# A hybrid attention, recurrence and expert block on one core: GpSimd's large two-operand operations go to VectorE

## The chip, the core and the metric

The kernel runs on one core of a Trainium2 chip, in one launch. The metric is the device time of that launch in microseconds (us). The engines are named as the profile names them: PE is TensorE, DVE VectorE, ACT ScalarE, POOL GpSimd, SP SyncE. The kernel before takes 1131.45 us, the median of three runs (1130.12 to 1132.07).

## What is computed

The reference is one layer over 272 tokens (16 learned meta tokens and 256 of the input) of width 1024, all in float32:

```python
h = layer_norm(concat([meta, x]), ln_emb_g, ln_emb_b)
qa, ka, va, qb, fb, ib, gb = split(h @ w_in)                  # 1024 x 3584
ya = diff_attention(qa, ka, va, lam, subln_g, ...)            # 4 heads, rotary, chunk-causal
yb = hgrn2(qb, fb, ib, gb, lb, norm_g)                        # 4 heads, gated linear recurrence
h = layer_norm(2**0.25 * h + concat([ya, yb]) @ w_out, ln1_g, ln1_b)
ffn = moe(h, ...)                                             # top 4 of 32 experts, clamped SwiGLU
return layer_norm(2**0.25 * h + ffn, ln2_g, ln2_b)[16:]
```

The weights of the 32 experts are 403 MB, and every expert has tokens, so all of them are read once.

## The kernel before

**The mixer stage.** `w_in` comes in 28 pieces and `w_out` in 8, each 128x1024 float32. `split` (L173) makes two float32r parts of a piece: ScalarE rounds it (`hi`, L178), and a second engine subtracts (`lo`, L180). That engine is VectorE for the even pieces from 4 on, and GpSimd for the others, 20 of 36. When `lo` is made, the piece's buffer is free, and the SP queue fetches the piece four further on (L183). There are three buffers for `hi` and for `lo`, so piece i+3 can be rounded when TensorE is done with piece i. `project` (L313) multiplies a piece with the 272 tokens in 24 matmuls. In between, by a list of steps written out by hand (`STEPS`, L50), stand the pieces of the recurrence (`diagonal`, `level 0` to `level 7`, `meta`), of the attention (`rope`, `scores`, `turn`, `out_a`), the norms of the heads (`norm`), and `mix`, which multiplies their outputs with the pieces of `w_out`.

The order of TensorE's instructions is that of the list. The order on the other engines is made by a scheduler, which places each instruction by its own estimate of when it can run; on the chip every engine then runs its queue in that order and waits where the head of the queue waits.

**What the change touches in it.** `split` (L180). `router_fold` (L276), which makes the low part of the experts' biases. `residual` (L291 and L292), which scales and shifts the two halves of the tokens, 128x1024 each, with rows eg and eb. `hg_level` (L418), which multiplies neighbouring decays into those of the next level; TensorE's L408 of the next level needs what L416 leaves. `rope` (L483), the product with the cosines. `affine` (L679 and L680), gain and shift of the norm ahead of the experts: whole rows (128x1024) for tokens 0 to 127, half rows (128x512) for tokens 128 to 255. Some small GpSimd operations of `hg_level` (L437, L439), the spreading of the bias selectors (L762) and two operations of the last norm stay on GpSimd.

**From the router to the experts.** `total1`, `turn1`, `logits`, `choose`, `affine`, `position` and `hot1` norm the tokens, choose experts and make the one-hot matrix G; `gather` (L715) multiplies G with the normed tokens, and the first expert's matmuls (L779) follow.

**The experts.** Each expert has six chunks of weights of 2 MB. Ten chunk buffers are there, six of them lent to the mixers as scratch at first. The SP queue issues all transfers in program order: ten chunks before the first expert, each when its buffer is free, the eleventh when the first expert's first chunk has been used, and so on.

Of the kernel before, what the change touches and what calls it, by code (L numbers as in the profile page):

```python
# [11 lines left out]
F32 = mybir.dt.float32  # L12
# [4 lines left out]
OP = mybir.AluOpType  # L17
PSUM = mybir.MemoryType.PSUM if hasattr(mybir, "MemoryType") else bass.MemoryType.PSUM

P = 128  # L20
# [3 lines left out]
L = T + NM  # L24
# [18 lines left out]
E_ROT, E_COS = 0, 128  # L43
# [85 lines left out]
def build(ctx, tc, x, meta, consts_d, mixc_d, vecs_d, rows_d, win_d, wout_d, wr_d, br_d, bgu_d, bdn_d, wexp_d, out):  # L129
    nc = tc.nc  # L130
# [17 lines left out]
    def bank(tag):  # L148
        return ps.tile([P, 512], F32, name="ps_" + tag, tag=tag, bufs=4 if tag == "s" else 2)

    def t1(name, shape=(P, L), dt=F32):
        return cpool.tile(list(shape), dt, name=name, tag="t1", bufs=T1)

    def t4(name, shape=(P, D), dt=F32):
        return cpool.tile(list(shape), dt, name=name, tag="t4", bufs=T4)


    h = cpool.tile([P, 2, D], F32, name="h")
    con = cpool.tile([P, NC_CONST], F32, name="con")
    vec = cpool.tile([P, NC_VEC], F32, name="vec")  # L160
    mixc = pool.tile([P, NC_MIX], F32, name="mixc")
# [4 lines left out]
    def fetch(i):  # L166
        t = pool.tile([P, 1024], F32, name="wraw", tag="raw", bufs=RAW)
        nc.sync.dma_start(t, win_d[i] if i < 28 else wout_d[i - 28])
        wraw[i] = t
# [3 lines left out]
    def split(i):  # L173

        raw = wraw.pop(i)
        hi = wpool.tile([P, 1024], F32R, name="whi", tag="hi", bufs=SPL)
        lo = wpool.tile([P, 1024], F32R, name="wlo", tag="lo", bufs=SPL)
        nc.scalar.copy(hi, raw)  # L178
        eng = nc.gpsimd if i < 3 or i % 2 else nc.vector
        eng.tensor_tensor(lo, raw, hi.bitcast(F32), op=OP.subtract)  # L180
        parts[i] = (hi, lo)
        if i + RAW < 36:
            fetch(i + RAW)  # L183
# [18 lines left out]
    bgu = cpool.tile([P, 2, 512], F32R, name="bgu")  # L202
# [5 lines left out]
    def row_bcast(r, name):  # L208
        t = t4(name)
        nc.sync.dma_start(t, bass.AP(tensor=rows_d.tensor, offset=rows_d.offset + r * D, ap=[[0, P], [1, D]]))  # L210
        return t
# [17 lines left out]
    for i in range(2):  # L229
        split(i)  # L230
# [34 lines left out]
    def router_fold(half):  # L265

        b = bank("g")
        if half == 0:
            nc.sync.dma_start(mixc, mixc_d)
            for k in range(KT):  # L270
                nc.tensor.matmul(b[0:1, 0:NE], vec[:, V_B1 + k:V_B1 + k + 1], wr[:, k, :], start=(k == 0),
                                 stop=(k == KT - 1))
            braw = t4("braw", (P, 2, 512))
            nc.sync.dma_start(braw, bgu_d)
            nc.scalar.copy(bgu, braw)
            nc.gpsimd.tensor_tensor(bgu[64:P], braw[64:P], bgu[64:P].bitcast(F32), op=OP.subtract)  # L276
            nc.vector.tensor_tensor(br, b[0:1, 0:NE], br, op=OP.add)
            nc.vector.tensor_tensor(wr, wr, vec[:, V_G1:V_G1 + 8][:, :, None].to_broadcast([P, KT, NE]), op=OP.mult)
            return
        nc.tensor.matmul(b[:, 0:NE], ones[0:1, :], br, start=True, stop=True)  # L280
        for k in range(KT):
            nc.tensor.matmul(b[:, NE:2 * NE], ones, wr[:, k, :], start=(k == 0), stop=(k == KT - 1))
        nc.vector.tensor_copy(brb, b[:, 0:NE])
        nc.vector.scalar_tensor_tensor(wr, b[:, None, NE:2 * NE].to_broadcast([P, KT, NE]), -1.0 / D, wr, op0=OP.mult,
                                       op1=OP.add)

    def residual():
        eg, eb = row_bcast(0, "eg"), row_bcast(1, "eb")
        rows["g1"], rows["b1"] = row_bcast(2, "g1"), row_bcast(3, "b1")
        for a in range(2):  # L290
            nc.gpsimd.tensor_tensor(h[:, a, :], h[:, a, :], eg, op=OP.mult)  # L291
            nc.gpsimd.tensor_tensor(h[:, a, :], h[:, a, :], eb, op=OP.add)  # L292

    rc, rings = [0], []

# [101 lines left out]
    def hg_level(lv):  # L397
        Kmf = Km.rearrange("p h t -> p (h t)")
        ATv = ATd.rearrange("p h a t -> p (h a) t")
        m = 1 << lv  # L400
        nb = T * 4 // (2 * m)
        Qv = Qf.rearrange("p (n u m) -> p n u m", u=2, m=m)
        Kv = Kf.rearrange("p (n u m) -> p n u m", u=2, m=m)
        b = bank("s")
        if m <= 64:
            for i in range(8):
                n0 = i * (64 // m)
                nc.tensor.matmul(b[:, i * 64:(i + 1) * 64], Kf[:, i * P:(i + 1) * P],  # L408
                                 Qv[:, n0:n0 + 64 // m, 1, :], start=True, stop=True)
        else:  # L410
            for hh in range(4):
                nc.tensor.matmul(b[:, hh * P:(hh + 1) * P], Kx[:, hh, 0:P], Qx[:, hh, P:T], start=True, stop=True)
        Tv = st["T"].rearrange("p (n u) -> p n u", u=2)
        nc.vector.tensor_tensor(Qv[:, :, 1, :], Qv[:, :, 1, :], Tv[:, :, 0:1].to_broadcast([P, nb, m]), op=OP.mult)
        if m <= 64:
            nc.vector.tensor_tensor(Kv[:, :, 0, :], Kv[:, :, 0, :], Tv[:, :, 1:2].to_broadcast([P, nb, m]), op=OP.mult)  # L416
            Tn = Tns[lv % 2][:, 0:nb]
            nc.gpsimd.tensor_tensor(Tn, Tv[:, :, 0], Tv[:, :, 1], op=OP.mult)  # L418
            st["T"] = Tn
        bv = b.rearrange("p (i t) -> p i t", t=64)  # L420
        if m <= 16:
            msk = mixc[:, E_MSK + lv * 64:E_MSK + (lv + 1) * 64].bitcast(I32)
            dst = ATv.rearrange("p i (n u m) -> p i n u m", u=2, m=m)[:, :, :, 1, :]
            nc.vector.copy_predicated(
                dst, msk.rearrange("p (n m) -> p n m", m=m)[:, None, :, :].to_broadcast([P, 8, 64 // m, m]),
                bv.rearrange("p i (n m) -> p i n m", m=m))
        elif m <= 64:
            for q in range(64 // m):
                nc.scalar.copy(ATv[q * 2 * m:q * 2 * m + m, :, q * 2 * m + m:(q + 1) * 2 * m],
                               bv[q * 2 * m:q * 2 * m + m, :, q * m:(q + 1) * m])  # L430
        else:
            nc.scalar.copy(ATx.rearrange("p h t -> p (h t)"), b)
        if m <= 8:
            nbm = 64 // (2 * m)
            Kmv = Kmf.rearrange("p (n u m) -> p n u m", u=2, m=m)
            Tmv = st["Tm"].rearrange("p (n u) -> p n u", u=2)
            nc.gpsimd.tensor_tensor(Kmv[:, :, 0, :], Kmv[:, :, 0, :], Tmv[:, :, 1:2].to_broadcast([P, nbm, m]), op=OP.mult)  # L437
            Tn = Tmns[lv % 2][:, 0:nbm]
            nc.gpsimd.tensor_tensor(Tn, Tmv[:, :, 0], Tmv[:, :, 1], op=OP.mult)  # L439
            st["Tm"] = Tn  # L440
# [36 lines left out]
    def rope(key, dst, m, n):  # L477
        s = rp.pop(key)
        c = bank("g")
        nc.tensor.matmul(c[:, 0:n], mixc[:, E_ROT:E_ROT + P], s[:, 0:n], start=True, stop=True)  # L480
        t = t1("rt")
        nc.vector.tensor_tensor(t[:, 0:n], c[:, 0:n], mixc[:, E_SIN + L - n:E_SIN + L], op=OP.mult)
        nc.gpsimd.tensor_tensor(s[:, 0:n], s[:, 0:n], mixc[:, E_COS + L - n:E_COS + L], op=OP.mult)  # L483
        nc.vector.tensor_tensor(dst[:, m, :], s[:, 0:n], t[:, 0:n], op=OP.add)

    os = {}
# [108 lines left out]
    def close():  # L595
        rawst.close()
        rings.append(ctx.enter_context(tc.tile_pool(name="ring2", bufs=1)))

    do = dict(project=lambda i: project(i, *posts[i]), split=split, prefetch=prefetch, fold=router_fold, residual=residual,
              diagonal=hg_diag, lam=lam, level=hg_level, meta=hg_meta, out_a=out_a, out_b=out_b, norm=fin, scores=scores,  # L600
              turn=a_turn, values_a=lambda m: v_turn("a", m), values_b=lambda m: v_turn("b", m), begin=begin, mix=mixin,
# [65 lines left out]
    g1, b1 = rows["g1"], rows["b1"]  # L667

    def affine(a):
        mu, rs = mus[a]  # L670
        ha = h[:, a, :]
        nmr = small.tile([P, 1], F32, name="nmr")
        nc.vector.scalar_tensor_tensor(nmr, mu, -1.0, rs, op0=OP.mult, op1=OP.mult)
        c0 = 512 if a else 0
        if a:
            nc.vector.scalar_tensor_tensor(ha[:, 0:c0], ha[:, 0:c0], mu, g1[:, 0:c0], op0=OP.subtract, op1=OP.mult)
            nc.vector.scalar_tensor_tensor(ha[:, 0:c0], ha[:, 0:c0], rs, b1[:, 0:c0], op0=OP.mult, op1=OP.add)
        nc.scalar.activation(ha[:, c0:], ha[:, c0:], AF.Identity, bias=nmr, scale=rs)
        nc.gpsimd.tensor_tensor(ha[:, c0:], ha[:, c0:], g1[:, c0:], op=OP.mult)  # L679
        nc.gpsimd.tensor_tensor(ha[:, c0:], ha[:, c0:], b1[:, c0:], op=OP.add)  # L680

    def weigh(a):
        nm = small.tile([P, 1], F32, name="nm")
# [499 lines left out]
```

## Time and profile before

| what | value |
|---|---|
| median of three runs | 1131.45 us |
| the profiled execution, its own time | 1132.66 us |
| its span, from the first instruction to the last | 1130.8 us |
| busy: PE, DVE, ACT, POOL | 1007.2, 337.3, 177.2, 99.2 us |
| bytes moved | 428.44 MB, mean 379 GB/s |
| mean granted TensorE clock | 0.963 |

The span is cut here in stages: the mixers up to about 183 us, the way from the router to the first expert up to 208 us, the experts, and the last norm. A busy share over the whole span hides that: GpSimd is busy for 99.2 us, nearly all of it in the first 200. The granted clock is a share of full speed; 1.0 is 2.4 GHz and 0.5 is 1.2 GHz.

### The profile page before, as it was taken

The page shows a single profiled execution, that of the slowest core. Times are in us where ns is not written, and L with a number is a line of the kernel's source. Part 1 is how long each engine was busy: PE and PEld are TensorE (multiplying, and loading weights), DVE is VectorE, ACT ScalarE, POOL GpSimd, SP SyncE. Part 2 cuts the span into 40 slices and gives each one's busy share as a digit, 9 for nine tenths or more (in the row PEclk, how much of TensorE's full clock was granted, in tenths as well). Part 3 has the DMA queues.
Part 4 walks back from the last instruction along what each step waited for, and adds up shares of the span by engine and source line. Part 5 has one row for each costly group of instructions (what it writes and reads, how often), then busy time and mean ns, then how long its engine had stood idle before and what let it go on. Part 6 is the DMA issues. An engine that isn't in the chain of part 4 may idle for free.

```text
span 1130.8 us, 14815 instructions
## 1 busy us (share of the span) xinstructions
PE 1007.2 (89%) x6066; PEld 525.7 (46%) x6067; DVE 337.3 (30%) x721; ACT 177.2 (16%) x394; POOL 99.2 (9%) x91
## 2 busy tenths in 40 slices
PE   5989898999769999999999999999976699866995
PEld 5988777443225534444444444444421345312432
DVE  6685878312102321222121222122220013200114
ACT  4424564111001001110110001000100001000102
POOL 3653314000000000000000000000000000000001
PEclk9999999999889999999999999999988899988998
DMA  6753468899999999999999999999999999999993
GB/s 216 268 216 109 160 223 304 340 416 400 426 428 427 427 429 427 427 427 427 428 427 426 428 429 427 427 428 428 428 426 427 428 428 429 424 429 427 428 409 129
DMA packets 37022, 428.44 MB, mean 379 GB/s; under 512 B 4388, under 2 KB 4772, under 8 KB 12758
## 3 DMA queue, kind: packets, MB, share of 16 engines
q1 hardware_dynamic: 36322, 426.71, 90.6%
q8 instruction: 50, 0.82, 0.3%
q10 hardware_dynamic: 628, 0.74, 0.2%
q14 instruction: 22, 0.18, 0.0%
HBM read 426.38 MB, written 1.05 MB: 378 GB/s over the span
## 4 chain that ended last, share of the span: by engine, by line
PE 71%; DMA 14%; DVE 6%; ACT 1%; issue 1%; POOL 0%; DVEq 0%; ACTq 0%; POOLq 0%
PE ps_pj L779 21%; DMA wchunk<-in_wexp 14%; PE ps_pj L793 10%; PE ps_s L715 5%; PE ps_pj L864 5%; PE ps_pj L319 4%; PE ps_s L828 4%; PE ps_pj L836 4%; PE ps_pj L828 4%; PE ps_s L897 3%; PE ps_pj L876 2%; PE ps_g L752 1%; PE ps_pj L774 1%; PE ps_s L408 1%; DVE acc L898 1%
## 5 line engine op out<-in xcount | busy, mean ns | idle before, releaser
L779 PE MATMUL ps_pj<-wchunk,XT 128*64 128x512 f32 x1088 | 245.2, 597 | 0.0
L742 DVE TENSOR_SCALAR g<-ps_pj 128x256 f32<-128x256 f32 x52 | 22.1, 425 | 512.5 <-PE ps_pj L779 243.6
L864 PE MATMUL ps_pj<-wchunk,XT 128*32 128x512 f32 x768 | 113.4, 685 | 39.2 <-DMA wchunk<-in_wexp 39.2
L779 PEld LDWEIGHTS ps_pj<-wchunk,XT 128*64 128x64 f32 x1088 | 73.4, 137 | 137.9 <-issue 137.6
L793 PE MATMUL ps_pj<-wchunk,at 128*64 128x256 f32 x1088 | 123.7, 382 | 1.6 <-DVE at L754 1.6
L743 ACT ACTIVATE sgm<-g 128x256 f32<-128x256 f32 x58 | 24.2, 416 | 497.8 <-DVE g L742 497.8
L793 PEld LDWEIGHTS ps_pj<-wchunk,at 128*64 128x64 f32 x1088 | 75.8, 137 | 43.0 <-issue 3.2
L319 PE MATMUL ps_pj<-c,whi 128*128 128x272 f32 (+1 forms) x420 | 84.8, 296 | 0.7 <-DVE c L241 0.4
L762 POOL CAST sel<-sels 128x128 fp32r<-128x128 f32 (+2 forms) x30 | 10.5, 349 | 841.9 <-PE ps_g L752 248.9
L864 PEld LDWEIGHTS ps_pj<-wchunk,XT 128*32 128x32 f32 x768 | 27.5, 122 | 118.0 <-issue 64.0
L715 PE MATMUL ps_s<-G,h 128*128 128x128 f32 (+1 forms) x480 | 61.7, 290 | 15.2 <-DVE G L697 13.9
L876 PE MATMUL ps_pj<-wchunk,at 128*32 128x256 f32 x768 | 58.1, 447 | 17.2 <-DMA wchunk<-in_wexp 8.3
L715 PEld LDWEIGHTS ps_s<-G,h 128*128 128x128 f32 x480 | 58.7, 203 | 27.2 <-DVE G L697 24.4
L319 PEld LDWEIGHTS ps_pj<-c,whi 128*128 128x128 f32 x420 | 68.2, 194 | 2.4 <-DVE c L241 0.8
L319 PE MATMUL ps_pj<-c,wlo 128*128 128x272 f32 (+1 forms) x224 | 64.7, 289 | 0.0
L180 POOL TENSOR_TENSOR wlo<-wraw,whi 128x1024 fp32r<-128x1024 f32 x20 | 51.4, 2573 | 60.6 <-ACT whi L178 60.6
L876 PEld LDWEIGHTS ps_pj<-wchunk,at 128*32 128x32 f32 x768 | 28.8, 127 | 43.2 <-issue 19.6
L897 PE MATMUL ps_s<-Y,C 128*128 128x512 f32 (+1 forms) x104 | 47.8, 602 | 0.0
L178 ACT CAST whi<-wraw 128x1024 fp32r<-128x1024 f32 x36 | 37.6, 1047 | 59.0 <-PE ps_pj L319 28.4
L799 ACT COPY Y<-ps_pj 64x256 f32<-64x256 f32 x68 | 24.9, 366 | 137.8 <-PE ps_pj L793 137.4
L319 PEld LDWEIGHTS ps_pj<-c,wlo 128*128 128x128 f32 x224 | 43.2, 193 | 0.0
L836 PE MATMUL ps_pj<-wchunk,at 128*128 128x512 f32 x96 | 42.2, 592 | 0.0
(293 smaller groups left out, 956.7 us busy)
## 6 DMA issues: line engine op xcount, KB each, us to landing
wchunk<-in_wexp SPq DMA_DIRECT2D x189, 2048.0 KB, 28.1
wraw<-in_win SPq DMA_DIRECT2D x28, 512.0 KB, 3.7
wchunk<-in_wexp SPq DMA_DIRECT2D x12, 512.0 KB, 17.4
wraw<-in_wout SPq DMA_DIRECT2D x8, 512.0 KB, 5.0
h<-in_x SPq DMA_DIRECT2D x4, 256.0 KB, 2.8
braw<-in_bgu SPq DMA_DIRECT2D x1, 512.0 KB
eg<-in_rows SPq DMA_DIRECT2D x1, 512.0 KB, 4.4
eb<-in_rows SPq DMA_DIRECT2D x1, 512.0 KB
```

What stands on the lines that cost most here:

```text
L178: nc.scalar.copy(hi, raw)
L180: eng.tensor_tensor(lo, raw, hi.bitcast(F32), op=OP.subtract)
L319: nc.tensor.matmul(b[:, 0:n], w[:, ks], v[:, L - n:L], start=(k == 0 and j == 0), stop=(k == KT - 1 and j == 2))
L715: nc.tensor.matmul(bs[k // 4][:, k % 4 * P:k % 4 * P + ns], h[:, a, k * P:(k + 1) * P], G[:, a].rearrange("p n w -> p (n w)"), start=(a == ...
L779: nc.tensor.matmul(gu[ab * 64:(ab + 1) * 64, :], X[:, kh * 4 + k, u * SL:(u + 1) * SL], wv[:, k, ab * 512:(ab + 1) * 512], start=False, st ...
L793: nc.tensor.matmul(dn[c][ab * 64:(ab + 1) * 64, 0:256], aTs[f // 4][:, f % 2, f // 2 % 2 * 64:f // 2 % 2 * 64 + 64], wv[:, f, ab * 256:(ab ...
L799: nc.scalar.copy(Y[u * 64:(u + 1) * 64, c * 512 + ab * 256:c * 512 + (ab + 1) * 256], dn[c][ab * 64:(ab + 1) * 64, 0:256])
L828: nc.tensor.matmul(gus[ab], X[:, kh * 4 + k, :], wv[:, k, ab * 512:(ab + 1) * 512], start=False, stop=(kh == 1 and k == 3))
L836: nc.tensor.matmul(dn[c], aT[f // 2][:, f % 2, :], wv[:, f, :], start=(f == 0), stop=(f == KT - 1))
L864: nc.tensor.matmul(gu[q * 32:(q + 1) * 32, :], X[:, kh * 4 + k, us], wv[q // 2][:, k, q % 2 * 512:(q % 2 + 1) * 512], start=False, stop=(k ...
L876: nc.tensor.matmul(dn[q * 32:(q + 1) * 32, 0:256], at[:, f % 2, f // 2 * 32:(f // 2 + 1) * 32], wv[q // 2][:, f, q % 2 * 256:(q % 2 + 1) * ...
L897: nc.tensor.matmul(o, C[:, a, :], Y[0:C.shape[0], cs], start=True, stop=True)
```

## The change

VectorE does these operations. Nothing else is edited. As the changed kernel has one line less in `split`, its line numbers are lower by one from there on.

```diff
@@ split
-        eng = nc.gpsimd if i < 3 or i % 2 else nc.vector
-        eng.tensor_tensor(lo, raw, hi.bitcast(F32), op=OP.subtract)
+        nc.vector.tensor_tensor(lo, raw, hi.bitcast(F32), op=OP.subtract)
@@ router_fold
-            nc.gpsimd.tensor_tensor(bgu[64:P], braw[64:P], bgu[64:P].bitcast(F32), op=OP.subtract)
+            nc.vector.tensor_tensor(bgu[64:P], braw[64:P], bgu[64:P].bitcast(F32), op=OP.subtract)
@@ residual
-            nc.gpsimd.tensor_tensor(h[:, a, :], h[:, a, :], eg, op=OP.mult)
-            nc.gpsimd.tensor_tensor(h[:, a, :], h[:, a, :], eb, op=OP.add)
+            nc.vector.tensor_tensor(h[:, a, :], h[:, a, :], eg, op=OP.mult)
+            nc.vector.tensor_tensor(h[:, a, :], h[:, a, :], eb, op=OP.add)
@@ hg_level
-            nc.gpsimd.tensor_tensor(Tn, Tv[:, :, 0], Tv[:, :, 1], op=OP.mult)
+            nc.vector.tensor_tensor(Tn, Tv[:, :, 0], Tv[:, :, 1], op=OP.mult)
@@ rope
-        nc.gpsimd.tensor_tensor(s[:, 0:n], s[:, 0:n], mixc[:, E_COS + L - n:E_COS + L], op=OP.mult)
+        nc.vector.tensor_tensor(s[:, 0:n], s[:, 0:n], mixc[:, E_COS + L - n:E_COS + L], op=OP.mult)
@@ affine
-        nc.gpsimd.tensor_tensor(ha[:, c0:], ha[:, c0:], g1[:, c0:], op=OP.mult)
-        nc.gpsimd.tensor_tensor(ha[:, c0:], ha[:, c0:], b1[:, c0:], op=OP.add)
+        nc.vector.tensor_tensor(ha[:, c0:], ha[:, c0:], g1[:, c0:], op=OP.mult)
+        nc.vector.tensor_tensor(ha[:, c0:], ha[:, c0:], b1[:, c0:], op=OP.add)
```

The scheduler places the moved instructions in VectorE's queue and shifts others around them. TensorE's queue is the same. Three places matter below.

The first is VectorE at the start, where the tokens' norm (L234 before, L233 now) hands over to the two parts of the normed tokens (L241 and L242, now L240 and L241), which the first matmuls need. Before:

```order
L222 RECIPROCAL rs_e<-sd_e 128x1
L218 BN_AGGR mv_e<-st_e 128x2
L234 TENSOR_SCALAR h<-h,mv_e,rs_e 128x1024
L222 RECIPROCAL rs_e<-sd_e 128x1
L234 TENSOR_SCALAR h<-h,mv_e,rs_e 128x1024
L241 CAST c_76<-h_184 128x272
L242 TENSOR_TENSOR c_76<-h_184,c_76 128x272
```

Now:

```order
L221 RECIPROCAL rs_e<-sd_e 128x1
L217 BN_AGGR mv_e<-st_e 128x2
L233 TENSOR_SCALAR h<-h,mv_e,rs_e 128x1024
L179 TENSOR_TENSOR wlo<-wraw,whi 128x1024
L221 RECIPROCAL rs_e<-sd_e 128x1
L233 TENSOR_SCALAR h<-h,mv_e,rs_e 128x1024
L179 TENSOR_TENSOR wlo<-wraw,whi 128x1024 x2
L240 CAST c_76<-h_184 128x272
L240 CAST c_76<-h_188 128x272
L241 TENSOR_TENSOR c_76<-h_184,c_76 128x272
```

The first three splits stand there now, one ahead of the second block of tokens and two ahead of the first cast.

The second is VectorE at level 0 of the recurrence, whose L416 (now L415) TensorE waits for (c_78 is the scratch that holds decays, keys and queries). Before:

```order
L180 TENSOR_TENSOR wlo<-wraw,whi 128x1024
L371 SCALAR_TENSOR_TENSOR c_78<-ps_pj,sgq 128x256
L391 TENSOR_TENSOR c_75<-ps_s,con 128x512 x2
L394 TENSOR_TENSOR c_78<-c_78 128x1024
L465 COPY vm<-ps_g 16x128
L466 COPY c_75<-ps_g 128x2x128
L180 TENSOR_TENSOR wlo<-wraw,whi 128x1024
L414 TENSOR_TENSOR c_78<-c_78 128x512
L263 SCALAR_TENSOR_TENSOR nlam<-le 128x1
L416 TENSOR_TENSOR c_78<-c_78 128x512
```

Now:

```order
L291 TENSOR_TENSOR h<-h,eb 128x1024
L290 TENSOR_TENSOR h<-h,eg 128x1024
L390 TENSOR_TENSOR c_75<-ps_s,con 128x512 x2
L393 TENSOR_TENSOR c_78<-c_78 128x1024
L179 TENSOR_TENSOR wlo<-wraw,whi 128x1024
L464 COPY vm<-ps_g 16x128
L465 COPY c_75<-ps_g 128x2x128
L291 TENSOR_TENSOR h<-h,eb 128x1024
L179 TENSOR_TENSOR wlo<-wraw,whi 128x1024
L262 SCALAR_TENSOR_TENSOR nlam<-le 128x1
L413 TENSOR_TENSOR c_78<-c_78 128x512
L415 TENSOR_TENSOR c_78<-c_78 128x512
```

Three of the four large operations of `residual` stand in this piece, and one split more.

The third is VectorE between the router's first logits (L647, now L646) and the choice of experts for tokens 0 to 127 (msk, L656, now L655), which TensorE's L662 waits for. Before:

```order
L218 BN_AGGR mv_l_1958<-st_l_1955 128x2
L649 MAX m_1907<-lgs 128x8
L676 SCALAR_TENSOR_TENSOR h<-h,mv_l_1958,g_649 128x512
L222 RECIPROCAL rs_l_1962<-sd_l_1960 128x1
L650 MAX_INDEX i_1978<-m_1907,lgs 128x8
L684 TENSOR_SCALAR nm<-m_1907 128x1
L673 SCALAR_TENSOR_TENSOR nmr<-mv_l_1958,rs_l_1962 128x1
L652 CAST f_1981<-i_1978 128x8
L677 SCALAR_TENSOR_TENSOR h<-h,rs_l_1962,b_651 128x512
L654 TENSOR_TENSOR eq<-con,f_1981 128x128
L656 TENSOR_REDUCE msk<-eq 128x32
```

Now:

```order
L678 TENSOR_TENSOR h<-h,g_649 128x1024
L221 RECIPROCAL rs_l_1962<-sd_l_1960 128x1
L648 MAX m_1907<-lgs 128x8
L679 TENSOR_TENSOR h<-h,b_651 128x1024
L649 MAX_INDEX i_1978<-m_1907,lgs 128x8
L672 SCALAR_TENSOR_TENSOR nmr<-mv_l_1958,rs_l_1962 128x1
L675 SCALAR_TENSOR_TENSOR h<-h,mv_l_1958,g_649 128x512
L651 CAST f_1981<-i_1978 128x8
L646 SCALAR_TENSOR_TENSOR lgs<-ps_g,rs_l_1962,brb 128x32
L653 TENSOR_TENSOR eq<-con,f_1981 128x128
L648 MAX m_1907<-lgs 128x8
L676 SCALAR_TENSOR_TENSOR h<-h,rs_l_1962,b_651 128x512
```

The two whole-row operations of `affine` now stand ahead of msk, which follows this piece directly; the two half-row ones follow msk and stand ahead of the first half of G (L703, now L702).

## Rows read from the trace of the kernel before

**Rows 1.** Stages: length; busy us of PE, PEld, DVE, ACT, POOL; granted clock, DMA share, GB/s.
```profile
105.00:156.00 51.00, 46.70 (x327) 39.55 (x326) 42.79 (x97) 26.17 (x67) 17.38 (x12) 1.00 0.43 151
156.00:183.00 27.00, 26.71 (x121) 19.97 (x120) 21.67 (x35) 13.74 (x31) 7.99 (x3) 1.00 0.71 252
183.00:208.00 25.00, 21.14 (x137) 16.81 (x136) 16.96 (x54) 7.48 (x16) 8.11 (x6) 0.86 0.82 333
...
212.00:1105.00 893.00, 806.87 (x4709) 357.74 (x4709) 173.38 (x405) 78.86 (x195) 10.46 (x30) 0.96 1.00 425
```

**Rows 2.** Timeline of the SP queue, 204 to 209 us: start, length, what.
```profile
208.12 0.33 SPq L309 DMA_DIRECT2D wchunk<-in_wexp  x1
```

**Rows 3.** Chain of waits around the first expert: start us, us, what.
```profile
204.50 3.58 PE ps_pj L779 x16
```

**Rows 4.** TensorE's waits up to 210 us: us in total, times, longest.
```profile
PE ps_g L540 <- DVE c L530: 3.9, 2, 3.0
PE ps_s L408 <- DVE c L416: 3.8, 3, 2.7
PE ps_g L662 <- DVE msk L656: 2.2, 1, 2.2
...
PE ps_pj L319 <- DVE hL L242: 1.7, 1, 1.7
```

**Rows 5.** Groups on VectorE by form: count, busy us, mean ns, idle before and its releaser.
```profile
L180 DVE TENSOR_TENSOR wlo<-wraw,whi 128x1024 fp32r<-128x1024 f32 x16 | 21.2, 1325 | 7.4 <-ACT whi L178 7.3
...
L414 DVE TENSOR_TENSOR c<-c 128x512 f32<-128x512 f32 x5 | 10.0, 1996 | 8.1 <-issue 4.2 <-PE ps_s L412 2.2 <-POOL h L292 1.7
...
L484 DVE TENSOR_TENSOR c<-c,rt 128x272 f32<-128x272 f32 x4 | 6.1, 1528 | 0.5 <-POOL c L483 0.4
...
L414 DVE TENSOR_TENSOR c<-c,Tn 128x512 f32<-128x512 f32 x3 | 2.0, 675 | 0.0
...
L394 DVE TENSOR_TENSOR c<-c 128x1024 f32<-128x1024 f32 x1 | 1.2, 1215 | 0.0
...
L234 DVE TENSOR_SCALAR c<-c,mv_e,rs_e 16x1024 f32<-16x1024 f32 x1 | 0.8, 784 | 0.0
```

**Rows 6.** Groups on GpSimd, the same columns.
```profile
L180 POOL TENSOR_TENSOR wlo<-wraw,whi 128x1024 fp32r<-128x1024 f32 x20 | 51.4, 2573 | 60.6 <-ACT whi L178 60.6
```

**Rows 7.** Groups on VectorE, 12 to 23 us, the same columns.
```profile
L241 DVE CAST c<-h 128x272 fp32r<-128x272 f32 x8 | 3.0, 411 | 1.2 <-ACT h L239 1.2
L242 DVE TENSOR_TENSOR c<-h,c 128x272 fp32r<-128x272 f32 x7 | 2.8, 440 | 0.0
L234 DVE TENSOR_SCALAR h<-h,mv_e,rs_e 128x1024 f32<-128x1024 f32 x1 | 2.6, 2553 | 0.0
L242 DVE TENSOR_TENSOR hL<-h,c 128x272 fp32r<-128x272 f32 x1 | 2.5, 2487 | 0.0
```

**Rows 8.** Timeline of VectorE and GpSimd, 53 to 64 us: start, length, what.
```profile
56.79 2.81 DVE L414 TENSOR_TENSOR c<-c 128x512 f32<-128x512 f32 x1
...
59.01 2.80 POOL L180 TENSOR_TENSOR wlo<-wraw,whi 128x1024 fp32r<-128x1024 f32 x1
...
59.52 2.30 DVE L263 SCALAR_TENSOR_TENSOR nlam<-le 128x1 f32<-128x1 f32 x1
```

**Rows 9.** Chain of waits, 58 to 80 us.
```profile
62.48 2.75 PE ps_s L408 x16
...
65.87 3.57 PE ps_pj L319 x24
...
70.38 2.00 PE ps_s L408 x16
72.37 2.90 PE ps_pj L319 x24
```

**Rows 10.** Timeline of VectorE, 184 to 206 us.
```profile
189.43 1.33 DVE L676 SCALAR_TENSOR_TENSOR h<-h,mv_l,g 128x512 f32<-128x512 f32 x1
...
190.97 2.02 DVE L673 SCALAR_TENSOR_TENSOR nmr<-mv_l,rs_l 128x1 f32<-128x1 f32 x1
```

## The prediction

> **What bounds the kernel now.** I read the engines by stage first. From 212 to 1105 us the DMA queues are full, share 1.00 at 425 GB/s, while TensorE is busy for 807 of 893 us [rows 1]: the transfers of the expert weights set that stage, and the change moves none of their bytes. So I looked for what starts this stream. The eleventh chunk is issued at 208.12 us [rows 2], just when the first expert's first 16 matmuls have freed a buffer (204.50 + 3.58 = 208.08) [rows 3]. All that follows hangs on that moment: **a microsecond by which TensorE gets there earlier or later is a microsecond of the kernel**, and the change can act only before it, since the operations that it moves all stand before it.
>
> Before it, TensorE is nearly full (46.7 of 51 us, then 26.7 of 27) [rows 1]. A faster or slower helper counts only where TensorE waits, and TensorE's waits name VectorE: 1.7 us for hL (L242) at the start, 3.8 for L416 in the recurrence, 3.9 for L530 in the attention, 2.2 for msk in the router [rows 4].
>
> Why VectorE is late there is to be seen in its groups. L414 on a 128x512 tile takes 675 ns three times, but 1996 ns as a mean of five others [rows 5]. At 59.52 us L263 works on one element per partition and takes 2.30 us; GpSimd's split of 2.80 us began at 59.01 and ends when L263 does [rows 8]. VectorE stood still until GpSimd was done. A GpSimd split takes 2573 ns, 20 times [rows 6]: each can hold VectorE that long.
>
> **The change part by part.** Prices on VectorE: L394, a product of the same 128x1024 shape and types of operand in SBUF, takes 1.215 us, and the 16 splits there a mean of 1.325 with some blocked among them [rows 5]. I take 1.2 for a split, for the bias part and for each whole-row operation, and 1.325 as the upper end; 0.68 for 128x512 (L414, unblocked) [rows 5], which also bounds each L418; 0.44 for a rope product (L242, 128x272) [rows 7]. In all VectorE gets 20 splits (24.0), the bias part (1.2), four in residual (4.8), eight L483 (3.5), affine (2 x 1.2 + 2 x 0.68 = 3.8) and seven L418 (under 4.8): 37 to 42 us. It gets back what it lost to blocking: five L414 (6.6) and four L484 (4 x 1.09 = 4.4) [rows 5], hL and one L234 (2.05 and 1.77) [rows 5, 7], L263 (2.1) [rows 8], L673 (1.9) [rows 10], and smaller ones. So VectorE's load grows by less than half of what is moved to it; what counts is the place.
>
> *Start.* On the way to the first project, L234 falls from 2.55 to 0.78 us and the last L242 from 2.49 to 0.44 [rows 5, 7]: 3.8 us less. Three splits come in (3.6). VectorE waits 1.2 us for ScalarE ahead of the first cast [rows 7], which takes in one of them, and the first split stands where VectorE waits for a deviation anyway; I put 1.8 on the path. **-2.0**, between -3.8 and 0.
>
> *Level 0 and 1 of the recurrence.* TensorE waits 2.7 us at L408, and 1.1 more in two later places [rows 4]. Ahead of that wait VectorE lost 2.1 us each in L414 and L263 (2.81 and 2.30) [rows 8], more than the wait. New in the queue are the four operations of residual and two splits, 7.2 us, but VectorE idles there too, and the bulk comes while TensorE still has two projects to do. I take the wait as down to 0.2: -2.5. The same blocking causes the later waits: -0.9. And after the long wait TensorE runs slower: L408 takes 2.75 us against 2.00 for the next one, the project 3.57 against 2.90 [rows 9]. Without the wait these 1.4 us go. **-4.8**; at the ends -5.2, and +2.0 if the six operations have no cover but the blocked time and half the rest. What would be late next is the next project, which has its split one project ahead.
>
> *Rope and scores, 105 to 156 us.* GpSimd's 12 instructions here [rows 1] are five splits and seven L483: 9.1 us come to an engine that is busy 42.8 of 51 [rows 1]. Four L484 give back 4.4 [rows 5]. Net 4.7, of which the 8.2 us of VectorE's idle time take most; in front of the turns of the heads (L540), where TensorE waits 3.9 us already [rows 4], I let about a fifth stay. **+1.0**, between 0 and 9.1. Here a page of the Trainium skill speaks against the change: Perfetto Trace Analysis, section Optimizing Scalar/DVE Operations, says that where the vector engine is saturated, handing work even to GpSimd can pay, though it adds that the shared read port may spoil it. By its first half all 9.1 us would land on the path here; that is the second rival.
>
> *Mix, 156 to 183 us.* Three splits (3.6) come to an engine with 5.3 us free, beside a TensorE that is busy 26.7 of 27 [rows 1]: 0. If the cover fails, they cost at most 3.6.
>
> *Router.* Two whole-row operations now stand ahead of msk (2.4) and two half rows between msk and G (1.4). L673 gives back 1.9 of its 2.02, L676 0.65 of its 1.33 (against 0.68) [rows 5, 10]. **+1.2**, between 0 and 3.8. The slow clock of this stage (mean 0.86 over 25 us, so 7 us of it at 1.2 GHz) [rows 1] I leave as it is.
>
> *Transfers.* A piece is fetched when its split is done, and 1.2 us frees it sooner than 2.6. The SP queue now issues the bias transfer one piece and the second expert chunk one piece earlier; a piece is needed three projects later, so 0.
>
> Sum: -2.0 - 4.8 + 1.0 + 1.2 = -4.6. Against the profiled execution's own 1132.66 that gives 1128.1; it ran 1.2 us above the median, so against 1131.45 I forecast **1126.9 us**.
>
> **Rivals.**
> 1. *The router takes the lead back.* If VectorE gets nothing back there, the four affine operations cost 3.8 us, and with TensorE idle for longer the gather stays at half speed for some 1.5 us more. -2.0 - 4.8 + 1.0 + 5.3 = -0.5: 1130.9. For it: TensorE already waits 2.2 us for msk [rows 4]. Against: L673 and L676 are plainly blocked.
> 2. *VectorE paces rope and scores: slower.* All 9.1 us land ahead of L530, and what blocking gives back lay beside other waits. -2.0 - 4.8 + 9.1 + 1.2 = +3.5: 1135.0. It decides from the point where TensorE's waits at L540 grow from 3.9 to over 10 us. For it: 84% busy [rows 1], and a queue in order that may stop at a split whose rounding isn't done. Against: 8.2 us of idle time and the L484.
> 3. *More is freed.* The L540 waits (3.9) go as well, and the router costs nothing: -2.0 - 4.8 - 3.9 = -10.7: 1120.8. For it: the four L484 are blocked in the stretch ahead of that wait [rows 5].
>
> **How the numbers follow.** Two kernels within 0.2% (2.3 us) of one another can hardly be told apart. The forecast's case gets 0.65 (its own range 1123 to 1130), rival 1 0.12, rival 2 0.10, rival 3 0.13. Faster by over 0.2% (below 1129.2): nearly all of the first and rival 3, 0.74. Within: rival 1 and the edge of the first, 0.15. Slower: rival 2 and a little of the rest, 0.11. The range 1121 to 1132 leaves out rival 2 and about half of rival 3.
>
> **What would show it.** Right: no VectorE operation of a few hundred ns that takes over 2 us before 200; VectorE's busy time up by less than 20 us and GpSimd's down by some 80; the hL wait below 0.5 us and the start 2 us earlier; the L408 waits below 0.5 in all and full clock between 60 and 70 us; the first expert's L779 at about 200 instead of 204.5, and the eleventh chunk 3.6 us after it; 893 us from there to the last chunk, as before. Wrong: L540 waits above 6 us (rival 2), msk and G later than 3 us after the router's logits compared with before (rival 1), a slow clock at a new place, or splits on VectorE of 2 us and more.

## The result, and the profile after

The changed kernel takes 1125.18 us, the median of four runs (1124.35 to 1126.05); the kernel before took 1131.76 in four runs beside it. The ratio on record is 0.9933, with a 95% interval of 0.9911 to 0.9955 (the two medians alone give 0.9942): **faster by 6.6 us**, a little more than the 4.6 that were forecast.

The engines by stage, in the changed kernel (columns as in [rows 1]):

```profile
105.00:156.00 51.00, 47.17 (x312) 39.34 (x311) 41.62 (x120) 27.51 (x77) 0.00 (x0) 0.97 0.52 177
156.00:183.00 27.00, 26.61 (x135) 21.64 (x134) 22.60 (x34) 12.62 (x23) 0.85 (x2) 1.00 0.75 270
183.00:208.00 25.00, 20.74 (x120) 13.55 (x120) 11.25 (x50) 5.78 (x13) 0.00 (x0) 0.80 0.75 303
212.00:1099.00 887.00, 803.61 (x4688) 358.72 (x4686) 171.04 (x399) 76.36 (x189) 10.53 (x30) 0.96 1.00 425
```

GpSimd is empty from 105 to 156 us, and yet VectorE is busy for 41.6 us there, where it was 42.8: it took over 12 operations and became no busier. (The change runs some 7 us ahead there. Between the same two instructions of TensorE, 105.1 to 154.6 us before and 97.0 to 147.6 after, VectorE is busy for 41.3 us before and for 40.3 after.) Over the whole span VectorE's busy time even fell, from 337.3 to 334.2 us. Its groups say why:

```profile
L179 DVE TENSOR_TENSOR wlo<-wraw,whi 128x1024 fp32r<-128x1024 f32 x36 | 43.7, 1216 | 15.2 <-ACT whi L178 15.2
...
L413 DVE TENSOR_TENSOR c<-c 128x512 f32<-128x512 f32 x5 | 3.4, 685 | 2.2 <-PE ps_s L411 1.8 <-PE ps_s L407 0.5
...
L483 DVE TENSOR_TENSOR c<-c,rt 128x272 f32<-128x272 f32 x4 | 1.7, 433 | 0.0
...
L679 DVE TENSOR_TENSOR h<-h,b 128x1024 f32<-128x1024 f32 x1 | 1.2, 1208 | 0.0
...
L241 DVE TENSOR_TENSOR hL<-h,c 128x272 fp32r<-128x272 f32 x1 | 0.4, 429 | 0.0
```

The five L413 (L414 before) take 685 ns in place of 1996, the four L483 (L484 before) 433 in place of 1528, and the last L241 429 in place of 2487 [rows 5, 7]. A split takes 1.216 us, where 1.2 was assumed. Up to 212 us, 17 operations of VectorE took more than 1.9 us before, and none does in the change.

TensorE's waits up to 212 us, to be held against [rows 4]:

```profile
PE ps_g L539 <- DVE c L529: 3.1, 2, 1.8
PE ps_s L714 <- DVE G L702: 2.1, 2, 1.5
PE ps_g L661 <- DVE msk L655: 1.9, 1, 1.9
...
PE ps_pj L318 <- DVE c L240: 0.5, 1, 0.5
```

The wait for hL (1.7) and those of the recurrence (3.8) are gone; the other two places stay, and the wait for G has got longer (1.3 before). The chain of waits runs on TensorE alone through the products of levels 1 and 2, which wait for what L415 of the level before leaves:

```profile
57.97 1.73 PE ps_s L407 x16
...
60.03 3.03 PE ps_pj L318 x24
63.06 1.73 PE ps_s L407 x16
64.79 2.86 PE ps_pj L318 x24
```

L407 and the project take 1.73 and 3.03 us where they took 2.75 and 3.57 behind the long wait [rows 9]. (Start, length, what; a piece that overlaps the one before it is cut at its start.)

Where the lead arises is to be seen by setting the same instruction of TensorE or SP in both traces side by side:

| point | before, us | after, us | lead, us |
|---|---|---|---|
| end of the first three projects | 28.82 | 26.97 | 1.85 |
| end of level 6's products (L408, now L407) | 91.86 | 83.79 | 8.07 |
| start of the last spreading of values ahead of the mix (L462, now L461) | 154.64 | 147.58 | 7.06 |
| end of the mix but for its last piece (L592, now L591) | 184.85 | 177.17 | 7.68 |
| eleventh chunk issued | 208.12 | 201.97 | 6.15 |
| last chunk issued | 1102.28 | 1096.16 | 6.12 |
| end of the span | 1130.83 | 1124.08 | 6.75 |

The eleventh chunk's issue in the timeline of the SP queue (start, length, what; two more issues are joined to it):

```profile
201.97 8.96 SPq L308 DMA_DIRECT2D wchunk<-in_wexp  x3
```

The lead at the eleventh chunk is carried through nearly 900 us of transfers to within 0.03 us; another 0.6 comes behind the last chunk. Each lead is that of one trace, and traces differ from the start: in the 14 at hand the first project begins between 14.1 and 15.3 us.

### The profile page after: what moved, and what is told of

It reads as the page before. It is cut to its first block, busy times and chain, and to the rows that moved or that the text cites. A ratio compares the mean times of both kernels' runs of the same rounds, so it can differ in the third digit from the quotient of the medians.

```text
span 1124.1 us, 14783 instructions
## 1 busy us (share of the span) xinstructions
PE 1008.5 (90%) x6066; PEld 529.2 (47%) x6067; DVE 334.2 (30%) x765; ACT 177.8 (16%) x394; POOL 20.1 (2%) x47
## 4 chain that ended last, share of the span: by engine, by line
PE 77%; DMA 14%; DVE 6%; issue 1%; ACT 1%; SPq 0%; DVEq 0%
PE ps_pj L778 21%; DMA wchunk<-in_wexp 14%; PE ps_pj L792 11%; PE ps_pj L318 7%; PE ps_s L714 6%; PE ps_pj L863 5%; PE ps_s L827 4%; PE ps_pj L835 4%; PE ps_pj L827 4%; PE ps_s L896 3%; PE ps_pj L875 2%; PE ps_g L751 1%; PE ps_pj L773 1%; PE ps_s L407 1%; DVE acc L897 1%
## 5 line engine op out<-in xcount | busy, mean ns | idle before, releaser
L179 DVE TENSOR_TENSOR wlo<-wraw,whi 128x1024 fp32r<-128x1024 f32 x36 | 43.7, 1216 | 15.2 <-ACT whi L178 15.2
L827 PE MATMUL ps_pj<-wchunk,XT 128*128 128x512 f32 x96 | 41.7, 592 | 0.0
```

The source lines that it names most:

```text
L179: nc.vector.tensor_tensor(lo, raw, hi.bitcast(F32), op=OP.subtract)
L827: nc.tensor.matmul(gus[ab], X[:, kh * 4 + k, :], wv[:, k, ab * 512:(ab + 1) * 512], start=False, stop=(kh == 1 and k == 3))
```

## The experiments

My theory: GpSimd's operations with two operands in SBUF hold VectorE, and what is held ahead of a TensorE wait is paid. The rival: GpSimd's work beside VectorE costs nothing in itself, and the change gained by shorter splits and another order. This table has, of each run, the time with its ratio to the kernel before on the same chip, and the issue of the eleventh chunk in its trace (208.12 before, 201.97 in the change). The kernel before took 1132.06 us beside runs 1 to 4, 1131.37 beside 5 to 8 and 1132.09 beside 9 to 12.

| run | median, us | ratio, 95% | eleventh chunk |
|---|---|---|---|
| 1 splits alone moved | 1128.39 | 0.9937 to 0.9978 | 204.13 |
| 2 all but the splits | 1134.96 | 0.9999 to 1.0031 | 211.54 |
| 3 affine back | 1123.74 | 0.9899 to 0.9948 | 196.13 |
| 4 rope back | 1122.50 | 0.9878 to 0.9935 | 200.97 |
| 5 filler, two operands | 1155.80 | 1.0178 to 1.0240 | 230.91 |
| 6 filler, one operand | 1154.99 | 1.0177 to 1.0226 | 231.53 |
| 7 filler, copies | 1127.12 | 0.9922 to 0.9974 | 203.24 |
| 8 residual back | 1128.50 | 0.9958 to 0.9988 | 203.59 |
| 9 affine late | 1123.43 | 0.9902 to 0.9935 | 199.90 |
| 10 the change again | 1123.89 | 0.9907 to 0.9944 | 201.23 |
| 11 64 fillers, two operands | 1140.09 | 1.0045 to 1.0096 | 212.64 |
| 12 64 fillers, one operand | 1130.59 | 0.9966 to 0.9996 | 207.80 |

**1. The splits alone.**

```diff
-        eng = nc.gpsimd if i < 3 or i % 2 else nc.vector
-        eng.tensor_tensor(lo, raw, hi.bitcast(F32), op=OP.subtract)
+        nc.vector.tensor_tensor(lo, raw, hi.bitcast(F32), op=OP.subtract)
```

> The kernel before with only the 20 splits moved to VectorE. Theory (VectorE was held by GpSimd's two-operand operations, and each held operation ahead of a TensorE wait paid it): the start gets its whole lead, 1.9 us, since splits alone held L234 and L242 there; at level 0 the wait at L408, 2.66 before, shrinks to about 1, since residual's operations on GpSimd still hold L414 but no split holds L263; the rope products still hold L484; affine stays as before. First expert about 4 us earlier than before, time 1127 to 1128. Rival (it is not the holding but the number of operations in VectorE's queue that decides): 24 us more on VectorE with most of the holding still there gives a wait of over 3 us at L408 or L540, and a time of 1131 or more.

The eleventh chunk comes 4.0 us sooner, as the theory had it (0.5 of them by an earlier start). It is luck that TensorE's clock leaves this number alone: it was halved from 131.1 to 138.0 us, which cost a project 2.3 us, so that the lead at the end of the mix is only 1.3 us. The rest comes in the router, where the waits are those of before and the gathers ran at the full clock, as the chain of waits shows:

```profile
194.22 2.02 PE ps_s L714 x16
...
197.34 2.05 PE ps_s L714 x16
```

Before, they took 2.71 and 3.79 us. The time is 0.4 above the forecast range, and the lead after three projects 2.5 us, again with the 0.5 of the start. Around level 0 TensorE's waits show more than the one that was forecast:

```profile
PE ps_s L388 <- DVE c L370: 2.7, 1, 2.7
PE ps_g L539 <- DVE c L529: 2.4, 1, 2.4
...
PE ps_s L407 <- DVE c L415: 1.6, 1, 1.6
```

The wait at L388, in `diagonal`, one step ahead of level 0, is new. The timelines of VectorE and of GpSimd in that stretch (start, length, what):

```profile
43.71 2.40 DVE L362 TENSOR_SCALAR Km<-sgn,olb 128x16 f32<-128x16 f32 x1
46.02 2.54 DVE L363 TENSOR_SCALAR c<-sgn,olb 128x256 f32<-128x256 f32 x1
48.48 2.06 DVE L179 TENSOR_TENSOR wlo<-wraw,whi 128x1024 fp32r<-128x1024 f32 x1
```

```profile
43.49 4.92 POOL L290 TENSOR_TENSOR h<-h,eg 128x1024 f32<-128x1024 f32 x2 [15.84 <-DVE wlo L179]
```

L362 works on 16 elements a partition and takes 2.40 us, beside `residual` on GpSimd, and two more operations behind it are long as well.

**2. All but the splits.** The changed kernel with the two lines of `split` as before.

> The changed kernel with the 20 splits back on GpSimd. Theory: no lead at the start (hL wait about 1.7 us again); the level 0 wait depends on splits that hold L413 or L415, 0.5 to 2 us; router as in the changed kernel, about 1.5 us lost. First expert 0 to 3 us earlier than before, time 1129 to 1132. If the parts simply add, its lead and that of the splits alone make up the whole lead of 6.2 us at the first expert. Rival (the parts work only together, since any two-operand operation left on GpSimd holds VectorE): the two leads make up less than 4 us.

The eleventh chunk comes 3.4 us later than before, where the theory allowed 0 to 3 us earlier, and the time is above its range too. The two halves of the change give 4.0 and -3.4, together 0.6 of the whole's 6.15. **The parts don't add.** The times agree, if narrowly: the ratios of runs 1 and 2 together make 0.9972, and the whole change has 0.9933, in run 10 0.9926. In run 2 the lead was lost between norm and the last turns of the heads: 2.0 us at 120, -2.8 at 157. About 2 of these 4.8 us are TensorE's clock, halved from 131.3 to 138.1 us: a project takes 5.18 us in the chain of waits, and 3.23 before.

```profile
133.74 5.18 PE ps_pj L319 x24
```

The rest are waits for VectorE. One of the places there, in the timelines of VectorE and then of GpSimd:

```profile
149.82 2.46 DVE L529 TENSOR_SCALAR c<-c,z 128x144 f32<-128x144 f32 x1
...
153.31 0.26 DVE L465 COPY vm<-ps_g 16x128 f32<-16x128 f32 x1
```

```profile
149.80 2.40 POOL L180 TENSOR_TENSOR wlo<-wraw,whi 128x1024 fp32r<-128x1024 f32 x1 [7.40 <-DVE z L528]
```

A split that began together with L529 held it to its end, and TensorE waits 1.1 us for the L465 behind it. VectorE has the work of rope here and is still held.

**3. Affine back.** In `affine`, the two products and sums on `nc.gpsimd` again.

> The changed kernel with only affine's gain and shift back on GpSimd. Theory (affine on VectorE costs 0.8 us at the first half of G and 1.1 us by the slow clock of the first gather): 1 to 2 us faster than the changed kernel at the first expert, time 1123.5 to 1124.5; L672 and L676 are held again (about 2 and 1.3 us), and the wait for msk is about 2.2 us. Rival (the slow clock comes from a place in time and not from affine): within 0.5 us of the changed kernel.

In time this kernel can't be told from the change (1123.74 against 1125.18 and, a second time, 1123.89). In its trace the waits in the router are as forecast, 2.2 us for msk and 1.3 in all for G, so 0.5 less than in the change (3.5 in place of 4.0), and L672 is held, in VectorE's timeline:

```profile
180.47 2.02 DVE L672 SCALAR_TENSOR_TENSOR nmr<-mv_l,rs_l 128x1 f32<-128x1 f32 x1
```

That trace reached the eleventh chunk 5.8 us sooner than the change, most of it for other reasons: its first project began 0.6 us earlier, and the clock was granted in full from 13.7 us on (19.7 in the change), not halved between 125 and 129, and halved for 3.4 us in the router, where it was for 10.2 in the change. What affine's place costs in waits is thus 0.5 us; what it costs in clock can't be told from one trace.

**4. Rope back.** In `rope`, the product with the cosines on `nc.gpsimd` again.

> The changed kernel with only the cosine products of rope back on GpSimd. Theory (the load on VectorE costs about 1 us between rope and the turns of the heads, by the wait of 0.6 us in norm and a slow clock after the 1.8 us wait at L539): with 3.5 us less on VectorE and up to 4.4 us of holding at L483 back, within 0.5 us of the changed kernel at 160 us. Rival (VectorE's load is what costs there, holding does not matter): 1 us or more faster.

At 147 us it leads the kernel before by 7.13 us, the change by 7.06: within 0.1, as the theory had it. But two things cancel there. TensorE's wait at the turns is shorter than the 3.1 us of the change, and the project behind it is slower, in TensorE's waits and in the chain of waits:

```profile
PE ps_g L539 <- DVE c L529: 2.4, 1, 2.4
```

```profile
126.46 5.38 PE ps_pj L318 x24
```

The clock was halved there for 6.8 us (124.4 to 131.3), and in the change for 3.4. So the eight products cost up to 0.7 us in waits for VectorE, which the longer slow clock hides at 147 us. The median, 1122.50, lies 2.7 us below that of the change, but the two intervals overlap: no gain is shown, and none is ruled out.

**5 to 7. GpSimd kept busy with work that nothing needs.** In the changed kernel, ahead of the load of the router's weights:

```diff
+    idle = con[:, C_IOTA:C_IOTA + 232].rearrange("p (a c) -> p a c", a=2)
+    for _ in range(128):
+        nc.gpsimd.tensor_tensor(idle, idle, ones[:, None, 0:116].to_broadcast([P, 2, 116]), op=OP.mult)
```

In run 6 the operation is `tensor_scalar(idle, idle, 1.0, None, op0=OP.mult)`, in run 7 `tensor_copy(idle, idle)`. The order on VectorE is that of the change (line numbers there are 3 higher).

> The changed kernel with 128 operations on GpSimd that nothing needs (a constant tile multiplied by ones in place, 128x232, two operands in SBUF), which run one after the other from the arrival of the constants on; the order on VectorE, TensorE and ScalarE is that of the changed kernel. Theory (a two-operand operation of GpSimd holds VectorE till its end): while they run, VectorE's operations with operands in SBUF each lose up to one filler operation, estimated 0.6 us from the 2.57 us of a 128x1024 split; splits take 1.5 us and more instead of 1.22, small operations of 0.1 us take 0.5, waits at L407 come back, the first expert is 3 us or more later than in the changed kernel. Rival (GpSimd's work beside VectorE costs nothing in itself; the change gained by faster splits and another order): durations and first expert as in the changed kernel, within 0.5 us.

> The same with one operand in SBUF (the tile times the number 1.0, in place). Theory, if holding needs two operands: VectorE's durations and the first expert as in the changed kernel, within 0.7 us. Rival (any GpSimd operation on SBUF holds VectorE): like the fillers with two operands, per microsecond of GpSimd's busy time.

> The same with a plain copy in place. Theory, if holding needs two operands: as in the changed kernel, within 0.7 us. Rival: as for the multiplication by a number.

VectorE's groups from 14 to 73 us, first with two operands, then with one, then with copies:

```profile
L179 DVE TENSOR_TENSOR wlo<-wraw,whi 128x1024 fp32r<-128x1024 f32 x11 | 15.4, 1408 | 3.5 <-ACT whi L178 3.5
...
L244 DVE TENSOR_TENSOR c<-h,c 128x272 fp32r<-128x272 f32 x7 | 6.1, 909 | 0.0
...
L265 DVE SCALAR_TENSOR_TENSOR nlam<-le 128x1 f32<-128x1 f32 x1 | 0.7, 659 | 0.0
```

```profile
L179 DVE TENSOR_TENSOR wlo<-wraw,whi 128x1024 fp32r<-128x1024 f32 x14 | 17.4, 1246 | 6.0 <-ACT whi L178 6.0
...
L244 DVE TENSOR_TENSOR c<-h,c 128x272 fp32r<-128x272 f32 x7 | 3.5, 529 | 0.0
...
L265 DVE SCALAR_TENSOR_TENSOR nlam<-le 128x1 f32<-128x1 f32 x1 | 0.1, 141 | 0.0
```

```profile
L179 DVE TENSOR_TENSOR wlo<-wraw,whi 128x1024 fp32r<-128x1024 f32 x13 | 16.5, 1270 | 5.3 <-ACT whi L178 5.3
...
L244 DVE TENSOR_TENSOR c<-h,c 128x272 fp32r<-128x272 f32 x7 | 4.0, 608 | 0.0
```

With two operands the 128x1 product L265 takes 659 ns in place of 141, and L244 909 in place of 429 (L241 in the change): each lost about 0.5 us, less than one filler. TensorE is 15.2 us late by 102 us. With one operand L265 is as in the change, L244 0.1 longer, and TensorE less than 0.7 us late up to the meta tokens' product (1.0 from the first project on, which began 0.4 sooner). Copies lie between: 0.18 us more for L244, and 1.3 at the eleventh chunk (2.1 from the first project on), outside the 0.7 that were forecast. Added up over VectorE's operations beside fillers up to 80 us, each against the same one in the change, the loss is 17.3 us with two operands (82 operations), 3.7 with one and 5.1 with copies (96 each). So the holding itself costs, and most of it takes two operands: the rival that GpSimd's company is free falls. The one that any of its work on SBUF holds as much falls too, though some cost stays. Nor does anything speak for a gain by shorter splits alone: in the trace before, no wait of TensorE up to 210 us names wlo, and the fillers take the gain back although the splits are on VectorE.

The *times* of 5 and 6 and their eleventh chunks tell nothing of it, since my edit had a wait of its own: the recurrence's small products on GpSimd stood behind the fillers, and TensorE waited 9.2 and 27.4 us for them.

**11 and 12. The same with 64 fillers**, `range(64)`.

> The changed kernel with 64 in place of 128 unneeded two-operand operations on GpSimd, so that GpSimd is free again before the meta tokens' product needs its small products. Theory (holding): by 0.95 us each they end near 74 us; VectorE's small operations take 0.6 us and more beside them; TensorE is 9 to 12 us later by then and stays so, and the first expert is as much later than in the changed kernel. Rival (what the 128 cost was the queue on GpSimd): within 1 us of the changed kernel.

> The same 64 with one operand in SBUF (times a number). Theory (only two operands hold VectorE; GpSimd waits for VectorE instead): they end near 75 us too, VectorE's durations stay within 0.1 us of the changed kernel's, and the first expert is within 1 us of it. Rival (busy time on GpSimd costs, whatever its operands): as with two operands, 9 us or more.

The fillers on GpSimd, two operands and then one:

```profile
L206 POOL TENSOR_TENSOR con<-con 128x232 f32<-128x232 f32 x64 | 68.3, 1067 | 17.6 <-DMA con<-in_consts 12.7
```

```profile
L206 POOL TENSOR_SCALAR con<-con 128x232 f32<-128x232 f32 x64 | 73.4, 1147 | 18.2 <-DMA con<-in_consts 13.0
```

With two operands the eleventh chunk is 10.7 us later than in the change, all of it lost by 80 us: as forecast, 68 us of such work cost 10.7. (The time is 15 us above the change's: this trace lost another 1.6 us between the eleventh chunk and the last and 2.2 behind it, for a cause that stays open.) With one it is 5.8 later, outside the forecast; but 3.5 of these are again the wait for GpSimd's small products, since its fillers ended at 92 us and not near 75. Up to that wait TensorE was 1 us late, and the other 1.3 are lost behind it, where the clock is halved (93.9 to 100.8 us). The forecast that GpSimd is the one that waits was right, and what follows from it I had not counted.

**8. Residual back.** In `residual`, its four operations on `nc.gpsimd` again.

> The changed kernel with only residual's four 128x1024 operations back on GpSimd, at level 0 of the recurrence. Theory: they hold VectorE's operations ahead of L415 (up to 2 us each for L413 and the splits), so 1 to 2 us of the wait at L407 come back although VectorE has 4.9 us less to do; a slower clock after it adds up to 1.4; first expert 1 to 3 us later than in the changed kernel. Rival (VectorE's load counts): no wait at L407 and the first expert within 0.5 us.

Its trace started 1.2 us sooner than the change's and was 2.8 us later after level 0's first L407: 4 us lost, though VectorE had 4.9 less to do. TensorE's waits:

```profile
PE ps_s L388 <- DVE c L370: 2.9, 1, 2.9
...
PE ps_s L407 <- DVE c L393: 0.7, 1, 0.7
```

The price was forecast for L407 alone, and most of it stands at L388, one step sooner, as in run 1. By the eleventh chunk it is 1.6 us behind the change; the time, 1128.50, is 3.3 us above that of the change, and above those of runs 3 and 4, which undo a part elsewhere.

**9 and 10. Affine late, and the change again.** In run 9 a factor of one, made from msk or psm, ties affine's first operations to the choice:

```diff
+        late_one = small.tile([P, 1], F32, name="late_one")
+        nc.vector.tensor_scalar(late_one, (psm if a else msk)[:, 0, 0:1], 0.0, 1.0, op0=OP.mult, op1=OP.add)
...
-        nc.vector.tensor_tensor(ha[:, c0:], ha[:, c0:], g1[:, c0:], op=OP.mult)
+        nc.vector.scalar_tensor_tensor(ha[:, c0:], ha[:, c0:], late_one, g1[:, c0:], op0=OP.mult, op1=OP.mult)
```

The mean that the half rows subtract is multiplied by the factor in the same way.

> The changed kernel, with affine's operations tied by a factor of one: those of tokens 0 to 127 to the choice of experts of these tokens, those of tokens 128 to 255 to their positions. So the choice (msk) stands ahead of both whole-row operations on VectorE, and the first half of G ahead of the four half-row ones. Theory (affine on VectorE costs by its place ahead of msk and G): the wait for msk goes from 1.9 to below 0.3 us, the first gather starts 2 to 3 us sooner after the last logits, the first expert is 2 to 4 us earlier than in the changed kernel, and the time 1121.5 to 1123.5. Rival (the same operations have to be done ahead of the gather anyway, in any order): the first expert within 1 us of the changed kernel.

> The changed kernel once more, beside the tied affine on the same chip. Theory: as before, first expert at 198 to 199 us, time 1124 to 1126. If the start of the execution varies, it shows as a constant shift from the first matmuls on.

Run 10 gives the change's ratio again, 0.9926, and its waits to a tenth from the first project on; its start is 0.7 us shorter. With that, its first expert (197.5) and its time (1123.89) lie just below what was forecast for them. In run 9 the first wait for msk is gone, in TensorE's waits:

```profile
PE ps_s L718 <- DVE G L706: 2.3, 2, 1.6
...
PE ps_g L661 <- DVE msk L655: 1.4, 1, 1.4
```

The 1.4 us left are for the second half's msk. The eleventh chunk comes 2.1 us sooner than in the change (2.6, less 0.5 by which its start was longer), as the theory had it, but not by its reason: the waits here are 3.7 us in all, where the change has 4.0. They only changed place, as the rival had it, and TensorE waits for VectorE's work in the router in either order. The other 2 us are clock: the first gather takes 2.05 us, and 3.78 in the change. The time doesn't show the lead, 1123.43 against 1123.89, and the profiled execution gives a reason for itself: from the eleventh chunk to the last it took 896.7 us, where 12 of the 14 traces at hand took 894.0 to 894.5 (run 11 took 895.8). Whether the longer stream belongs to the edit or to that execution stays open. No run here beats the change clearly.

## Why the prediction was right, and where it was off

**The bound.** The first expert's start is what counts: the lead of 6.15 us at the eleventh chunk is that at the last chunk. In twelve traces with eleventh chunks from 196 to 232 us the stream took the same time to within 0.5 us; in runs 9 and 11 it took 2.5 and 1.6 us longer.

**VectorE's load** was to grow by less than half of the 37 to 42 us moved to it. It fell by 3.1, while GpSimd's fell from 99.2 to 20.1: what was held was as much as what was moved.

**Start, -2.0 forecast: -1.85.** Of this 0.27 stands ahead of the first project, less than the 1.2 us by which traces differ there. The hL wait of 1.65 is gone, and the one for the first cast went from 0.4 to 0.5 only: the three splits ahead of it found cover.

**Recurrence, -4.8 forecast: -6.2.** The mechanism was right, and this is the mis-sized term: it holds most of the 1.6 us by which the sum fell short at the eleventh chunk. The wait for level 0's L416 went from 2.66 to nothing (I left 0.2), the later ones from 1.1 to nothing (I left 0.2). The half clock cost 1.7 and not 1.4, since I had not counted the two spreading products between L408 and the project (0.63 us before, 0.38 after). The other 0.7 are steps below 0.3 us each that no wait names. Most of the term is residual's: with it left on GpSimd, waits of 4.3 (run 1) and 3.6 us (run 8) stand at the diagonal and level 0, and run 2, which moves it and leaves the splits, goes from 0.6 us behind at the end of the first three projects to 3.2 ahead at the end of level 2's products. The upper end of this term, +2.0, doesn't come out of its own words: 7.2 us of new work less 4.2 of blocked time, and half of the rest, are 1.5.

**Rope and scores, +1.0 forecast: +1.0,** by another way than I gave. I let a fifth of the load stay at the turns. In waits, rope's part of it costs up to 0.7 us there (run 4; that of the five splits was not tried alone in the changed kernel), but what was freed is more, and the waits at the turns fell from 3.9 to 3.1. A wait of 0.6 in norm came in, and a project at a halved clock took 4.6 us in place of 3.2, in the chain of waits of the change:

```profile
125.91 4.61 PE ps_pj L318 x24
```

In runs 3 and 8 the clock stayed full in this place beside the same two waits, 1.8 and 1.3 us long. A slow clock at a new place was named as a sign against the prediction, and here it is, in both traces of the change (run 10 too). What decides between the two clocks stays open. Without the slow one the term would be about -0.4, so that the sum of this place came out by luck.

**Mix, 0 forecast: -0.6,** the 0.27 wait at L592 and some shorter steps.

**Router, +1.2 forecast: +1.5,** and this is right by two errors. In waits the four operations cost 0.5 us and not 1.2 (0.3 less for msk, 0.8 more for G). The other 1.1 are the first gather, which ran at 1.2 GHz throughout: I had left the clock as it was. In the chain of waits, before and then now:

```profile
195.50 2.71 PE ps_s L715 x16
```

```profile
188.35 3.78 PE ps_s L714 x16
```

Rival 1 had put a slower gather at 1.5 us, a price that none of its rows gives. I had also put the cost down to the place ahead of msk, and run 9 shows that with this place free the waits are 3.7 in place of 4.0 us.

**The rivals.** The router didn't take the lead back (1.5 of 7.7 us). VectorE doesn't pace rope and scores in the changed kernel: the waits at L539 are 3.1 us and not over 10. The rule of the Trainium skill that was weighed there (Perfetto Trace Analysis, Optimizing Scalar/DVE Operations) finds little support here in its first half: beside a VectorE that is busy for 82% of that stretch, rope's work handed to GpSimd took 0.7 us off the waits at L539 and showed no gain in time that its interval separates from the change (run 4). Its second half agrees with runs 5 and 11, which show that two-operand work on GpSimd holds VectorE; that it is a port which they share, no run here shows. Rival 2 is real, in part, in another kernel: in run 2, where VectorE has rope's work and is still held by splits, this stretch took 4.8 us more, some 2 of them by the clock. More was freed than forecast, but not by the way of rival 3: the waits at L539 stay.

**What fell in my theory** is that the parts add. Each place was right to within 1.4 us for the whole change, but in run 2 one half of it by itself puts the eleventh chunk 3.4 us later, some 2 of them by the clock, and in ten runs of that kernel no gain is left.

## What to carry to other kernels

Look at VectorE's groups by shape for means far above those of the same shape elsewhere, and then for a two-operand GpSimd operation that ends with them; the work moved to VectorE costs little when it gives back what it was held for. What is left behind can hold the work that was moved as well: with the splits left on GpSimd nothing was gained (run 2), with residual less than half (run 8), while affine or rope left there cost nothing that the times show (runs 3 and 4). So try the parts alone and together. If GpSimd must work beside a busy VectorE, give it operations with one operand in SBUF, and let nothing urgent queue behind them.

## What the runs showed of the hardware

- Holding goes both ways. The two-operand filler takes 0.67 us at its shortest and 0.95 as a mean of 128. With one operand VectorE is hardly held (141 ns stays 141, 429 become 529), and it is GpSimd that is stretched: 0.79 us at its shortest, 1.15 as a mean of the 64 that lie beside VectorE's work. In GpSimd's timeline of run 5 and then of run 6, a filler of either kind with VectorE out of its way:

```profile
111.57 0.67 POOL L206 TENSOR_TENSOR con<-con 128x232 f32<-128x232 f32 x1
```

```profile
115.47 0.79 POOL L206 TENSOR_SCALAR con<-con 128x232 f32<-128x232 f32 x1
```

- The same stretch with the same waits is granted a full clock in one kernel's trace and a half in another's (125 to 129 us: 1.0 in runs 3 and 8, halved for 3.4 us in the change and in runs 9 and 10, with waits of 1.8 and 1.3 us in all five), which is worth 1.4 us at one place. The kernels differ elsewhere, and whether one and the same kernel shows both was not seen. Two kernels whose traces differ by less than that can't be ranked by one trace.
